# A second level of Strassen's scheme inside the product P3 of each two groups (first products of both SwiGLUs, and the projections)

## The chip, the cores and the metric

The kernel runs on one core of one Trainium2 chip. The metric is the device time of one execution in microseconds; the number given is the median of three runs. A core has a matrix engine (TensorE: PE for its matmuls, PEld for its weight loads), a vector engine (VectorE: DVE), a scalar engine (ScalarE: ACT), and queues that start DMA transfers (here all on SyncE: SP). Each engine works through its own list of instructions in order, and semaphores hold an instruction back until what it needs is there. Matmuls add up in PSUM, eight banks of 128 x 512 fp32; everything else lies in SBUF.

## What is computed

One layer on 1024 tokens of width 1024, in fp32: a SwiGLU with a half-weight residual, a mixing sub-layer (retention and pooling branches behind one combined projection, then gates and an output projection), a second SwiGLU, and a final norm.

```
h = h + 0.5 * swiglu_ffn(rmsnorm(h, norm_ffn1), ffn1_w_in, ffn1_w_out)
u = rmsnorm(h, norm_mix)
proj = u @ w_in                      # 1024 -> 7168: q, k, v, g_ret, p, gates
...                                  # rotary, retention, pooling, gates
h = h + merged @ w_out
h = h + 0.5 * swiglu_ffn(rmsnorm(h, norm_ffn2), ffn2_w_in, ffn2_w_out)
out = rmsnorm(h, norm_final)

def swiglu_ffn(x, w_in, w_out):      # 1024 -> 2 * 2816 -> 1024
    gate, up = jnp.split(x @ w_in, 2, axis=-1)
    return (jax.nn.silu(gate) * up) @ w_out
```

## The kernel before

**Tiling.** Activations lie transposed: channels on the 128 partitions, 1024 tokens along the free dimension. A product takes a 128x128 block of weights as the stationary operand and 512 tokens as the moving one. Every fp32 operand is split into a high and a low part: `split` lets ACT write the high part (a cast, L146) and DVE the rest (L147); `mm3` (L166 to L168) then issues three matmuls, high x high, high x low, low x high. So one 128x128 block on 512 tokens is three matmuls of 128x512.

**Groups and Strassen.** The first products of the SwiGLUs (`ffn_in`) and the projections (`projections`) are cut in groups of 2 x 128 output rows: gate and up of one slice, or two slices of a projection. A group is the product of a 2x2 matrix of weight blocks (L11, L12, L21, L22, each 512 channels in, 128 out) with a 2x2 matrix of activation blocks (R11, R12, R21, R22, each 512 channels by 512 tokens). `strassen` computes it by the Winograd form: seven products in place of eight, P1 to P7, each of 4 x 3 = 12 matmuls of 128x512. Its sums of weights are S1 = L21 + L22, S2 = S1 - L11, S3 = L11 - L21 and S4 = L12 - S2, made on DVE (L365) for every group; the sums of activations T1 to T4 are made once for a stage by the class `Next`, and all seven operands of a stage (4 tiles each) stay in SBUF, in 28 buffers with the tag "mv". The product P3 = S4 x R22 is the last term of one quarter of the result: it is added in PSUM to what bank `b` holds (`b3`), and the bank is then read out by `evac((0, 1), ...)`: on DVE with the factor of the norm (L527 in the SwiGLUs), or by ACT as a copy.

**Order.** `in_turn` yields the steps of the groups: the first two groups of a stage product by product in alternation, the others one after another in the order P1, P7, P6, P2, P5, P4, P3. The first SwiGLU begins with one group without Strassen (`plain_group`). `Flow.run` calls a step's preparation (loads, sums, splits of weights) four steps ahead of its matmuls; after each step it takes one or two pieces of background work (`flow.add`: norm factors, gates, rotary, stores) from a queue. A scheduler then puts the instructions of each engine in a fixed order. All DMAs stand in the one queue of SP, in order.

**Buffers.** PSUM: six banks with the tag "ps" (`bank`) and two with the tag "sum" (`sum_bank`); `b` is a "sum" bank, `a` and `e` are "ps" banks. SBUF: five split weights ("wt"), four raw weight tiles ("raw"), nine tiles of 128x1024 ("t4"), four more ("tl"), eight of 128x512 ("c2"). The "tl" tiles are used by `ffn_out` for the operands that it loads back (`p1` loads `R[k]` into one), by the rotary tables, and by the retention units for q, k and v.

Of the kernel before, what the change touches and what calls it, by code (L numbers as in the profile page):

```python
# [48 lines left out]
N_PS, N_SUM, N_IDLE = 6, 2, 6  # L49
# [40 lines left out]
def block_kernel(ctx: ExitStack, tc, x, x_tok, vecs, f1_in, f1_out, w_in, pool_w, w_ret, w_pool, w_o,  # L90
# [156 lines left out]
    class Next(Norm):  # L247


        def __init__(self, name, gain, keep=None):  # L250
            super().__init__(name)
            self.gain, self.keep = gain, keep
            self.M, self.tiles, self.t1s, self.rb = {}, {}, {}, None
# [70 lines left out]

        def work(self, *steps):

            for f in steps:
                for i in range(4):
                    flow.add(lambda f=f, i=i: f(i))
# [23 lines left out]
    def strassen(nx, wa, wb, name, evac, end, begin=None):  # L353
# [13 lines left out]
        def prep_w(n):  # L367
            def go():
                if n == "L11":
                    blocks()  # L370
                elif n == "S2":
                    combine("S1", "L21", "L22", ADD)
                    combine("S2", "S1", "L11", SUB)
                elif n == "S3":
                    combine("S3", "L11", "L21", SUB)
                elif n == "S4":
# [60 lines left out]
        def last(f):  # L437
            def go():
# [7 lines left out]
        return [(prep_w("L11"), b1), (prep_w("S2"), b6), (prep_w("S1"), b5), (prep_w("S3"), b7),  # L446
                (prep_w("L12"), b2), (prep_w("S4"), last(b3)), (prep_w("L22"), last(b4))]

    def in_turn(groups, order=range(7), first=2):

        groups = list(groups)
        steps = [g() for g in groups[:first]]
        for n in order:
            for g in steps:
                yield g[n]

        for g in groups[first:]:
            steps = g()
            for n in (0, 3, 1, 4, 2, 6, 5):
                yield steps[n]  # L460
# [18 lines left out]
    def plain(M, nk, src, name, evac, begin=None):  # L479

        t = {}
        for q in range(0, nk, 4):
# [27 lines left out]
    def ffn_in(nx, w, ops, name, start=None):  # L510
# [3 lines left out]

        def group(g):
            gate_up = []

            def evac(which, in0, in1):
                if not gate_up:
                    new = tl if start and g == 0 else t4  # L520
                    gate_up.extend((new(f"{name}g{g}"), new(f"{name}u{g}")))
                tile, j = which
                dst = half(gate_up[tile], j)
                if in1 is not None:
                    tt(dst, in0, in1, ADD)
                elif nx.rb is not None:
                    tt(dst, in0, half(nx.rb, j), MUL)  # L527
                    return
                else:
                    copy(dst, in0)  # L530
                flow.add(lambda: tt(dst, dst, half(nx.rms(), j), MUL))

            def end():
# [5 lines left out]
                def times(j):  # L539
                    tt(half(up, j), half(gate, j), half(up, j), MUL)  # L540

                flow.add(swish, lambda: times(0), lambda: times(1))
                hid[g] = up
# [3 lines left out]
                lo, hi, e = hid.pop(k), up, {}  # L547
                R11, R12, R21, R22 = half(lo, 0), half(lo, 1), half(hi, 0), half(hi, 1)

                def w1():  # L550
                    e["n"], e["m"] = t4(f"{name}n{k}"), c2(f"{name}m{k}")
                    tt(half(e["n"], 0), R12, R11, SUB)
                    tt(half(e["n"], 1), R22, R12, SUB)
                    load(B[k], e["n"])

                def w2():
                    tt(R12, R22, half(e["n"], 0), SUB)
# [3 lines left out]
                def w3():  # L561
                    tt(e["m"], R21, R12, SUB)
# [7 lines left out]
            return lambda: strassen(nx, w[g, 0], w[g, 1], f"{name}{g}_", evac, end)  # L570
# [3 lines left out]
        if start:  # L574
            return chain(group(0), in_turn((group(g) for g in order[1:]), (0, 4, 1, 2, 3, 5, 6)))
        return in_turn((group(g) for g in order), BY_OPERAND)
# [237 lines left out]
    first.work(first.r11, first.r21, first.r12, first.r22, first.p22, first.t2, first.t1, first.t3, first.t4_)  # L814
# [9 lines left out]
    first.stats(x_sums)  # L824

# [14 lines left out]
    def end_of(nx):  # L840
        def end(part):
            if part == 0:
                nx.work(nx.r11, nx.r22, nx.t2, nx.t1, nx.t3, nx.p22)
            else:
                nx.work(nx.r21, nx.t4_)
                nx.stats()
# [11 lines left out]
    def rotary_tables():  # L858
        for n, z in (("cos", 0), ("sin", 1)):
            raw_t = tl(f"{n}raw")  # L860
            load(raw_t, rope[z])
            tab[n] = t4(n)
            tt(tab[n], raw_t, mix.rms(), MUL)

    def project(kind, n):
# [87 lines left out]
        def end():  # L953
            if kind in "qk":
                flow.add(*rotate(0), *rotate(1), lambda: keep(qs if kind == "q" else ks))
                if (kind, n) == heavy[-1]:
                    flow.add(units[0].loads)
# [8 lines left out]
        return lambda: strassen(mix, w_in[at], w_in[at + 1], name, evac, end)  # L966
# [5 lines left out]
    def projections():  # L972
        for n, step in enumerate(in_turn(project(*o) for o in order)):
            if n == 28:
# [7 lines left out]
    def pool(n):  # L982
# [12 lines left out]
        def body():  # L995
            for i in range(2):
                mt = 2 * n + i
                dst = [f(f"px{mt}{j}") for j, f in enumerate((sum_bank, bank))]
# [214 lines left out]
    def retention():  # L1213
# [7 lines left out]

        yield units[0].operands, units[0].values
# [34 lines left out]
    def after(nx):  # L1257
# [5 lines left out]
        return {0: nx.r11, 4: nx.r21, 1: t2, 3: nx.t3, 2: nx.t1, 6: nx.t4_, 5: nx.p22}  # L1263
# [75 lines left out]
    def merge():  # L1339
        yield from two_by_two(two_groups(0) + two_groups(1), BY_OPERAND, handed(mg, lambda rest: flow.add(*rest)))  # L1340
        yield from two_by_two((out_group(i) for i in range(4)), BY_OPERAND,
                              handed(ffn2, lambda rest: (flow.add(*rest[:4]), ffn2.stats(between=rest[4:]))))
# [117 lines left out]
```

## Time and profile before

| | |
|---|---|
| median of 3 runs | 2192.77 us (2190.7 to 2193.43) |
| the profiled execution | 2192.35 us, of which its span is 2190.6 us |
| ACT busy | 985.3 us (45%) |
| DMA | 311.86 MB, mean 142 GB/s |
| mean granted TensorE clock | 0.997 |

The page gives each engine's busy time, a picture of the span in 40 slices, the chain of work that ended last and the costliest groups. In a group, the name left of the arrow is what is written; then come the shape, the count, the busy time, the mean duration of one and the idle time ahead of it. The stages by the tiles' names: first SwiGLU 0 to 644 us (its first products to 434), projections 644 to 1175, retention and pooling to 1386, merge and output projection to 1541, second SwiGLU from there on (its first products to 1964). In the names, `a` and `c` are the groups of the two SwiGLUs' first products, `n1`, `n2`, `n3` their operands and those of the projections, `b` and `d` their second products.

### The profile page before, as it was taken

The page shows a single profiled execution, that of the slowest core. Times are in us where ns is not written, and L with a number is a line of the kernel's source. Part 1 is how long each engine was busy: PE and PEld are TensorE (multiplying, and loading weights), DVE is VectorE, ACT ScalarE, POOL GpSimd, SP SyncE. Part 2 cuts the span into 40 slices and gives each one's busy share as a digit, 9 for nine tenths or more (in the row PEclk, how much of TensorE's full clock was granted, in tenths as well). Part 3 has the DMA queues.
Part 4 walks back from the last instruction along what each step waited for, and adds up shares of the span by engine and source line. Part 5 has one row for each costly group of instructions (what it writes and reads, how often), then busy time and mean ns, then how long its engine had stood idle before and what let it go on. Part 6 is the DMA issues. An engine that isn't in the chain of part 4 may idle for free.

```text
span 2190.6 us, 27454 instructions
## 1 busy us (share of the span) xinstructions
PE 2171.6 (99%) x10070; PEld 1809.5 (83%) x10070; DVE 1677.5 (77%) x2766; ACT 985.3 (45%) x1756; POOL 0.2 (0%) x4
## 2 busy tenths in 40 slices
PE   9999999999999999999999999999999999999998
PEld 7788888888888888888888998878888888888887
DVE  8687777887786767677776777799977777689775
ACT  8433333444553433434336664446533333344451
POOL 0000000000000000000000000000000000000000
PEclk9999999999999999999999999999999999999999
DMA  6144222495323333323235557524242323249522
GB/s 239 58 154 168 92 104 96 162 334 178 125 92 112 139 116 116 115 105 127 96 124 187 188 180 278 192 87 147 75 144 101 135 92 123 94 158 337 173 73 78
DMA packets 111015, 311.86 MB, mean 142 GB/s; under 512 B 12448, under 2 KB 14624, under 8 KB 110880
## 3 DMA queue, kind: packets, MB, share of 16 engines
q1 hardware_dynamic: 110880, 310.11, 40.0%
q8 instruction: 79, 1.29, 0.2%
q14 instruction: 56, 0.46, 0.1%
HBM read 219.36 MB, written 90.70 MB: 142 GB/s over the span
## 4 chain that ended last, share of the span: by engine, by line
PE 94%; DVE 3%; ACT 2%; DMA 1%; issue 0%; SPq 0%; DVEq 0%; ACTq 0%
PE c_b L166 3%; PE c_b L168 3%; PE c_b L167 3%; PE a_b L168 2%; PE a_b L166 2%; PE a_b L167 2%; PE c_e L166 2%; PE c_a L167 2%; PE c_a L166 2%; PE c_a L168 2%; PE c_e L168 2%; PE c_e L167 2%; PE a_e L168 2%; PE a_e L167 2%; PE a_a L168 2%; PE a_e L166 2%
## 5 line engine op out<-in xcount | busy, mean ns | idle before, releaser
L146 ACT CAST c_wS<-c_S 128x512 fp32r<-128x512 f32 x88 | 54.7, 622 | 124.7 <-PE c_b L168 76.1
L146 ACT CAST a_wS<-a_S 128x512 fp32r<-128x512 f32 x84 | 52.2, 622 | 105.7 <-PE a_b L168 71.0
L147 DVE TENSOR_TENSOR c_wS<-c_S,c_wS 128x512 fp32r<-128x512 f32 x88 | 60.9, 692 | 22.6 <-ACT c_wS L146 22.0
L147 DVE TENSOR_TENSOR a_wS<-a_S,a_wS 128x512 fp32r<-128x512 f32 x84 | 58.2, 693 | 24.4 <-ACT a_wS L146 24.0
L167 PE MATMUL c_a<-n3R,c_wL 128*128 128x512 f32 x176 | 68.6, 390 | 0.0
L167 PE MATMUL c_b<-n3T,c_wS 128*128 128x512 f32 x176 | 68.5, 389 | 0.0
L168 PE MATMUL c_b<-n3T,c_wS 128*128 128x512 f32 x176 | 68.5, 389 | 0.0
L168 PE MATMUL c_a<-n3R,c_wL 128*128 128x512 f32 x176 | 68.5, 389 | 0.0
L166 PE MATMUL c_a<-n3R,c_wL 128*128 128x512 f32 x176 | 68.3, 389 | 0.0
L166 PE MATMUL c_b<-n3T,c_wS 128*128 128x512 f32 x176 | 68.2, 389 | 0.0
L168 PE MATMUL a_a<-n1R,a_wL 128*128 128x512 f32 x168 | 65.4, 389 | 0.0
L166 PE MATMUL a_a<-n1R,a_wL 128*128 128x512 f32 x168 | 65.4, 389 | 0.0
L167 PE MATMUL a_a<-n1R,a_wL 128*128 128x512 f32 x168 | 65.4, 389 | 0.0
L166 PE MATMUL a_b<-n1T,a_wS 128*128 128x512 f32 x168 | 65.4, 389 | 0.0
L167 PE MATMUL a_b<-n1T,a_wS 128*128 128x512 f32 x168 | 65.4, 389 | 0.0
L168 PE MATMUL a_b<-n1T,a_wS 128*128 128x512 f32 x168 | 65.4, 389 | 0.0
L146 ACT CAST c_wL<-c_ra 128x512 fp32r<-128x512 f32 x44 | 27.2, 620 | 38.0 <-PE c_e L168 38.0
L146 ACT CAST a_wL<-a_ra 128x512 fp32r<-128x512 f32 x42 | 26.0, 621 | 37.6 <-PE a_e L168 37.6
L167 PEld LDWEIGHTS c_a<-n3R,c_wL 128*128 128x128 f32 x176 | 33.0, 188 | 7.2 <-DVE n3R L151 0.3
L167 PEld LDWEIGHTS c_b<-n3T,c_wS 128*128 128x128 f32 x176 | 33.0, 188 | 7.0 <-DVE n3T L151 0.2
L147 DVE TENSOR_TENSOR c_wL<-c_ra,c_wL 128x512 fp32r<-128x512 f32 x44 | 30.4, 692 | 10.8 <-ACT c_wL L146 10.5
L168 PEld LDWEIGHTS c_a<-n3R,c_wL 128*128 128x128 f32 x176 | 33.0, 188 | 6.9
(2500 smaller groups left out, 7300.3 us busy)
## 6 DMA issues: line engine op xcount, KB each, us to landing
c_ra<-in_f_in SPq DMA_DIRECT2D x22, 512.0 KB, 3.7
c_rb<-in_f_in SPq DMA_DIRECT2D x22, 512.0 KB, 4.7
a_ra<-in_f_in SPq DMA_DIRECT2D x21, 512.0 KB, 4.5
a_rb<-in_f_in SPq DMA_DIRECT2D x21, 512.0 KB, 5.1
t<-au SPq DMA_DIRECT2D x11, 512.0 KB, 2.6
b<-an SPq DMA_DIRECT2D x11, 512.0 KB, 3.2
r<-au SPq DMA_DIRECT2D x11, 512.0 KB, 3.8
br<-r SPq DMA_DIRECT2D x11, 512.0 KB, 5.4
```

The lines of the kernel that those rows point to most:

```text
L146: copy(hi, src)
L147: tt(lo, src, hi.bitcast(F32), SUB)
L166: mm(dst, w[0], m[0], start=start, stop=False, skip_group_check=True)
L167: mm(dst, w[0], m[1], start=False, stop=False, skip_group_check=True)
L168: mm(dst, w[1], m[0], start=False, stop=stop, skip_group_check=True)
```

## The change

Two groups A and B now share their P3. S4 of A and S4 of B, one above the other, are a 2x2 matrix of blocks (2 groups x 2 halves of the channels, each 256 in and 128 out), R22 is one of 2 x 2 blocks of 256 channels by 256 tokens, and their product is made by the same Winograd form again: seven products, each of 2 x 3 = 6 matmuls of 128x256. Before, the two P3 were 24 matmuls of 128x512; now they are 42 of 128x256.

- **Weights** (`third`): S4 itself is no longer split. Split are S4 of A (`wx`), two pairs of sums (`ws12`, `ws34`, from four DVE operations of 128x256, L507 to L514) and half of S4 of B (`wy`).
- **Operands** (`Next.quads`): x00, x10, x01, x11 are the quarters of R22, y1 = x01 - x00, y2 = x11 - y1, y4 = x10 - y2, y3 = x11 - x01. They take the place of the four split tiles of R22. Three lie in "mv"; x00, x10, y1 and x11 take all four "tl" buffers for the whole stage, x01 one of "t4".
- **Partial sums**: the products x00, y1 go to a bank `x`, y2 and y3 to a bank `y`, x10 and x11 straight onto bank `b` of A, y4 onto bank `b` of B. ACT copies x00's half of `x` to `y`, and `y`'s one half to its other, between the products; DVE and ACT collect the rest in two SBUF tiles `z` (L529 to L552), which `evac((0, 1), b, z)` adds on the way out (DVE, L663), the norm's factor following as an operation of its own.
- **Order**: `pairs` yields A's six other products, B's six, and then the three steps of `third` with 18, 12 and 12 matmuls. The first pair of a stage goes in alternation as before. In the first SwiGLU the plain group, nine pairs, one group alone (`third_alone`: P3 as 24 matmuls of 128x256 on the four quarters) and one pair; 14 pairs in the projections, 11 in the second SwiGLU: 35 pairs.
- **Elsewhere**: five "ps" banks and three "sum" banks; the pooling products write two "sum" banks instead of one of each; the first group's gate and up lie in "mv"; the rotary tables are loaded straight into "t4"; the first retention unit loads q, k and v at the start of the retention, behind which two pooling products stand, no longer during the projections; the preparation of R22 as an operand is gone from the projections and the second SwiGLU.

```diff
-N_PS, N_SUM, N_IDLE = 6, 2, 6
+N_PS, N_SUM, N_IDLE = 5, 3, 4
...
+        def quads(self):
+            both = [slice(z * HD, (z + 1) * HD) for z in range(2)]
+            x = {(i, j): [self.tiles[4 + 2 * i + z, 1][:, both[j]] for z in range(2)] for i in range(2) for j in range(2)}
...
+            return [block(0, 0), block(1, 0), difference("y1", (0, 1), (0, 0)), difference("y2", (1, 1), "y1"), block(1, 1),
+                    difference("y4", (1, 0), "y2"), difference("y3", (1, 1), (0, 1))], block(0, 1)
...
+        def prep1():
+            w["x"] = weights(a["S4"], f"{A.name}wx")
+            s = t["s"] = c2(f"{A.name}s12")
+            tt(s[:, LO], b["S4"][:, LO], b["S4"][:, HI], ADD)
+            tt(s[:, HI], s[:, LO], a["S4"][:, LO], SUB)
+            w["s12"] = weights(s, f"{A.name}ws12")
...
+        def prod(dst, n, at, m, start=False):
+            for z in range(2):
+                mm3(dst, parts(w[n], at + z), nx.quad(m, z), start and z == 0, z == 1)
+
+        def one():
+            x, y = t["x"], t["y"] = bank(f"{A.name}x"), sum_bank(f"{A.name}y")
+            a["z"], b["z"] = c2(f"{A.name}z"), c2(f"{B.name}z")
+            prod(x[:, LO], "x", 0, "x00", True)
+            with soon():
+                copy(y[:, LO], x[:, LO])
+                copy(a["z"][:, LO], x[:, LO])
+            prod(a["b"][:, LO], "x", 2, "x10")
+            prod(x[:, HI], "s12", 0, "y1")
+            with soon():
+                copy(b["z"][:, HI], x[:, HI])
+
+        def two():
+            y = t["y"]
+            prod(y[:, LO], "s12", 2, "y2")
+            with soon():
+                copy(y[:, HI], y[:, LO])
+                tt(a["z"][:, HI], y[:, LO], b["z"][:, HI], ADD)
+            prod(a["b"][:, HI], "s34", 2, "x11")
+            with soon():
+                A.third()
+
+        def three():
+            y = t["y"]
+            prod(b["b"][:, LO], "y", 0, "y4")
+            prod(y[:, HI], "s34", 0, "y3")
+            with soon():
+                copy(b["z"][:, LO], y[:, HI])
+                tt(b["z"][:, HI], y[:, HI], b["z"][:, HI], ADD)
+                B.third()
...
-                    t["dst"] = [f(f"{name}d{j}") for j, f in enumerate((sum_bank, bank))]
+                    t["dst"] = [sum_bank(f"{name}d{j}") for j in range(2)]
...
+        yield units[0].loads, none
+        yield from fill(2)
         yield units[0].operands, units[0].values
```

Three places where the change moves rows. The rows are the fixed order of one engine, with the semaphores that a row waits for; the numbers at the names tell buffers apart.

On PE, in a pair in the middle of the second SwiGLU, P3 of one group before (bank `b`, operand R22 in four `n3R` tiles):

```order
L166 MATMUL c_b<-n3R_13424,c_wS_14723 128x512 [waits DVE_49]
L167 MATMUL c_b<-n3R_13424,c_wS_14723 128x512
L168 MATMUL c_b<-n3R_13424,c_wS_14723 128x512
L166 MATMUL c_b<-n3R_13427,c_wS_14723 128x512
L167 MATMUL c_b<-n3R_13427,c_wS_14723 128x512
```

and now the middle of the first step of `third` at that place: the end of x10 (`n3x_14726`, onto bank `b`), the first matmul of y2 (`n3y_14770`, onto bank `y`), and y1 (`n3y_14757`, onto the second half of bank `x`):

```order
L167 MATMUL c_b<-n3x_14726,c_wx 128x256
L168 MATMUL c_b<-n3x_14726,c_wx 128x256
L166 MATMUL c_y<-n3y_14770,c_ws_16007 128x256 [waits Activation_49]
L166 MATMUL c_x<-n3y_14757,c_ws_16007 128x256 [waits Activation_49]
L167 MATMUL c_x<-n3y_14757,c_ws_16007 128x256
L168 MATMUL c_x<-n3y_14757,c_ws_16007 128x256 [waits DVE_49]
```

The scheduler has put one matmul of y2 ahead of y1; both wait for ACT, where P3 waited for no one between its matmuls.

On ACT, at that same place, now (`c_wL`, `c_wS` are weights of the next pair):

```order
L146 CAST c_wL_16066<-c_ra 128x512 [waits DMAHW4_49,PE_49,Activation_49]
L529 COPY c_y<-c_x 128x256 [waits PE_49]
L530 COPY c_z<-c_x 128x256
L146 CAST c_wS_16085<-c_S_16083 128x512 [waits DVE_49,PE_49,Activation_49]
L534 COPY c_z<-c_x 128x256 [waits PE_49]
L540 COPY c_y<-c_y 128x256 [waits PE_49]
```

Four copies, of which the first, second and fourth stand between PE's products; before, ACT had nothing to do between the matmuls of a P3. The order is the same in all pairs but the first of a stage.

On SP, at the end of the first SwiGLU's first products, the loads for `ffn_out` now (`br` is the "tl" tile of `p1`, `bra` and `bL22a` are weights):

```order
L134 DMA bra_4030<-in_f_out 128x1024 [waits DMAHW4_49,DVE_49]
L134 DMA bra_4083<-in_f_out 128x1024 [waits DMAHW5_49,DVE_49]
L134 DMA br_3964<-r_123 128x1024 [waits DMAHW6_49,PE_49]
L134 DMA br_4028<-r_124 128x1024 [waits DMAHW7_49,PE_49]
L134 DMA br_4081<-r_125 128x1024 [waits DMAHW0_49,PE_49]
L134 DMA br_4142<-r_126 128x1024 [waits DMAHW1_49,PE_49]
```

and before, the piece with the fifth of these loads, the first that waits for a buffer:

```order
L134 DMA bra_3555<-in_f_out 128x1024 [waits DMAHW0_49,DVE_49]
L134 DMA br_3712<-r_126 128x1024 [waits DMAHW1_49,DVE_49]
L134 DMA bra_3603<-in_f_out 128x1024 [waits DMAHW2_49,DVE_49]
L134 DMA bL22a_3605<-in_f_out 128x512 [waits DMAHW6_49,DMAHW7_49,DMAHW3_49,DVE_49]
L134 DMA bra_3671<-in_f_out 128x1024 [waits DMAHW5_49,DVE_49]
```

Before, the first four `br` stood far ahead of this piece, since nothing else held the four "tl" buffers; now the first four wait for PE, for the last pair's x00, x10, y1 and x11 to be done.

More of the change, by code (lines that the diff above doesn't have):

```diff
@@ L462, in two_by_two, with alone @@
+    def alone(nx, group):
+        A = group()
+        for m in BY_SUM:
+            yield A[m]
+        yield third_alone(nx, A)
     def two_by_two(groups, order, between=None):
@@ L824, in block_kernel @@
     first.stats(x_sums)
+    quads, x01 = first.quads()
+    flow.add(*quads, x01)
     ops1 = spill("r", FH), spill("t", FH), spill("b", FH), spill("m", FH, H)
@@ L972, in projections @@
     def projections():
[L973 to L974 removed]
+        for n, step in enumerate(pairs(mix, (project(*o) for o in order), (0, 1, 2, 3, 4, 6))):
+            if n == 30:
                 flow.rate = 1
```

132 lines of the change are left out of this document (95 added, 37 removed).

## Prediction

> **What bounds the kernel now.** First the page: the span, the busy times and the chain that ended last.
>
> ```profile
> span 2190.6 us, 27454 instructions
> PE 2171.6 (99%) x10070; PEld 1809.5 (83%) x10070; DVE 1677.5 (77%) x2766; ACT 985.3 (45%) x1756; POOL 0.2 (0%) x4
> PE 94%; DVE 3%; ACT 2%; DMA 1%; issue 0%; SPq 0%; DVEq 0%; ACTq 0%
> ```
>
> PE is busy for 99% of the span, and 94% of the chain is PE's. So a matmul less is time less, as long as nothing else becomes late. Who could become late is read from the three stages that change, in the view of windows (us, then the busy time of PE, PEld, DVE, ACT and POOL, each with its number of instructions, PE's granted clock, the DMA share, GB/s):
>
> ```profile
> 0.00:434.00 434.00, 429.50 (x1875) 352.25 (x1876) 330.20 (x529) 192.40 (x315) 0.20 (x4) 1.00 0.37 132
> 644.00:1175.00 531.00, 531.00 (x2347) 438.96 (x2346) 384.63 (x605) 216.05 (x379) 0.00 (x0) 1.00 0.32 118
> 1541.00:1964.00 423.00, 423.00 (x1869) 348.97 (x1868) 323.30 (x512) 166.65 (x271) 0.00 (x0) 1.00 0.31 110
> ```
>
> PE has no gap in two of them (531.00 of 531.00, 423.00 of 423.00) and 4.5 us in the first. The clock is whole. DVE is next: 323.30 of 423 us in the second SwiGLU, 76%. ACT has room. DVE decides whether the change pays.
>
> **The change: matmuls.** The gain hangs on what a matmul of half the width costs. The timeline of PE (start, duration, instruction) shows a run of the full width, and two runs of the half width, from other stages:
>
> ```profile
> 1759.79 0.39 PE L166 MATMUL c_e<-n3T,c_wS 128*128 128x512 f32 x1
> ...
> 1760.24 0.39 PE L168 MATMUL c_e<-n3T,c_wS 128*128 128x512 f32 x1
> 1760.47 0.39 PE L166 MATMUL c_b<-n3T,c_wS 128*128 128x512 f32 x1
> 2155.05 0.28 PE L168 MATMUL dp6b<-dp4m,dp4w 128*128 128x256 f32 x1
> ...
> 2165.49 0.28 PE L168 MATMUL dp6b<-dp4m,dp4w 128*128 128x256 f32 x1
> 1193.01 0.28 PE L166 MATMUL ob<-v,sm 128*128 128x256 f32 x1
> ...
> 1194.93 0.28 PE L168 MATMUL ob<-v,sm 128*128 128x256 f32 x1
> ```
>
> The spacing counts, not the duration, since matmuls are pipelined. Full width: 0.68 us for three steps, 0.2267 each. Half width: 10.44 us for 87 steps of an output product, 0.120; 1.92 us for 17 steps in the retention, 0.113. So the half is a little more than half. I take 0.118, near the long run.
>
> The order of PE loses 852 matmuls of 128x512 (35 pairs x 24, and 12 of the group that is alone) and gains 1494 of 128x256 (35 x 42 + 24). Removed: 852 x 0.2267 = 193.1 us. Added: 1494 x 0.118 = 176.3. **Balance -16.8 us**; -13.8 at 0.120, -24.3 at 0.113. A pair goes from 24 x 0.2267 = 5.44 us to 42 x 0.118 = 4.96: a gain of 0.48, out of 168 x 0.2267 = 38.1 us.
>
> The Trainium skill, page "TensorE: Matmul & The Clock Gate", section "Back-to-back issue gap", gives for a single matmul N / 2.4 + 2.5 ns, which would be 215.8 ns at 512 and 109 at 256, an estimate of 183.9 - 162.8 = 21 us from that page. The rows show 226.7 and 113 to 120, so the measurement decides.
>
> **y1 waits for ACT.** x00 goes to one half of bank `x`, y1 to the other, and in the fixed order y1 stands behind both copies that ACT makes of x00. What such a step costs is read at other hand-overs (the first ACT row follows the c_e row of 1760.24 above):
>
> ```profile
> 1760.67 0.59 ACT L419 COPY c_p<-c_e 128x512 f32<-128x512 f32 x1 [1.61 <-PE c_e L168]
> 1761.15 0.62 ACT L146 CAST c_wS<-c_S 128x512 fp32r<-128x512 f32 x1
> 1195.53 0.69 ACT L146 CAST state<-sf 128x512 fp32r<-128x512 f32 x1
> 1196.27 0.19 PEld L166 LDWEIGHTS xb<-state,q 128*128 128x128 f32 x1 [1.26 <-ACT state L146]
> 1196.27 0.38 PE L166 MATMUL xb<-state,q 128*128 128x256 f32 x1 [1.06 <-ACT state L146]
> ```
>
> ACT starts 0.04 us after the recorded end of the last matmul (1760.24 + 0.39 = 1760.63). A second ACT instruction starts 0.11 before the first one's end (1760.67 + 0.59 = 1761.26, next 1761.15). PE starts 0.05 after ACT's end (1195.53 + 0.69 = 1196.22, then 1196.27), and the first matmul after a wait takes 0.38 instead of 0.28. A copy of 256 columns out of PSUM is not in the trace; it is bounded by its neighbours (groups: count, busy, mean ns, idle before):
>
> ```profile
> L397 ACT COPY c_b<-c_a 128x512 f32<-128x512 f32 x22 | 12.6, 571 | 21.6 <-PE c_a L168 21.6
> L402 ACT COPY c_v<-c_b 128x512 f32<-128x512 f32 x22 | 12.9, 587 | 27.4 <-PE c_b L168 27.4
> L146 ACT CAST c_wS<-c_S 128x512 fp32r<-128x512 f32 x88 | 54.7, 622 | 124.7 <-PE c_b L168 76.1
> L146 ACT CAST sm<-sc 128x256 fp32r<-128x256 f32 x8 | 3.3, 407 | 4.9 <-DVE sc L1105 4.9
> ```
>
> A cast loses 622 - 407 = 215 ns by halving; so 571 - 215 = 0.36 us for the copy to `y`, 587 - 215 = 0.37 for that to `z`.
>
> Now with x00's start as 0: its sixth matmul starts at 5 x 0.118 = 0.59 and ends at 0.87; copy y from 0.91 to 1.27 (the cast of `wL` ahead of it on ACT is done by then); copy z from about 1.18 to 1.55; y1's weights from 1.60. Without a wait y1 would start after x00, x10 and the one matmul of y2 that stands ahead: 13 x 0.118 = 1.53. With the 0.1 of a first matmul that is 1.70 against 1.53, **0.16 us** per pair in round figures. At 33 pairs in steady order (35 without the first ones of two stages) that is **+5.3 us**. From below 0 (a faster copy), from above 0.35 us (each copy a full 0.57, without overlap nearly twice that, but y2's matmul hides part): 0 to 11.5 us. What is behind the wait: all of PE, so it counts in full.
>
> The Trainium skill, page "PSUM — Partial Sum Buffer", section "PSUM bank collisions raise a hardware error", says that two engines may not be on one bank at once even at different columns. That speaks against putting x00 and y1 on one bank: without the rule y1 need not wait, the term is 0 and the time 2178.5. No run here shows a collision; the wait stands in the order all the same.
>
> **DVE's additions.** The prices, by groups and one pair of neighbours:
>
> ```profile
> L147 DVE TENSOR_TENSOR c_wS<-c_S,c_wS 128x512 fp32r<-128x512 f32 x88 | 60.9, 692 | 22.6 <-ACT c_wS L146 22.0
> L147 DVE TENSOR_TENSOR sm<-sc,sm 128x256 fp32r<-128x256 f32 x8 | 3.4, 423 | 0.2
> L527 DVE TENSOR_TENSOR cg<-c_b,n3rb 128x512 f32<-128x512 f32 x22 | 15.2, 691 | 13.0 <-PE c_b L168 12.9
> 1761.80 0.69 DVE L147 TENSOR_TENSOR c_wS<-c_S,c_wS 128x512 fp32r<-128x512 f32 x1 [1.42 <-ACT c_wS L146]
> 1762.41 0.68 DVE L365 TENSOR_TENSOR c_S<-c_ra,c_rb 128x512 f32<-128x512 f32 x1
> ```
>
> Per pair come one split of 512 (0.69) and one of 256 (0.42), six sums of 256 (6 x 0.42 = 2.5), and two more read-outs of 512, since adding `z` and multiplying by the norm's factor are two operations (2 x 0.69): 5.0 us. The operands of `quads` add 7.1 us to a stage. In the second SwiGLU DVE then needs 323.3 + 11 x 5.0 + 7.1 = 385 of 418 us, 92%. I cost this at nothing, because the order puts DVE's work ahead of its use. The nearest date inside the third is y3, which needs the sum of L541, since that reads the other half of bank `y`. In DVE's order six operations lead up to it, of which the first, an evac, starts when PE is done with `e`, at 0.2 (x00's start is 0): five spacings of 0.61 us (1761.80 to 1762.41) and its own 0.42 make it ready at 3.7, and 4.0 with a wait for a cast; PE needs it after 36 matmuls and y1's wait, at 36 x 0.118 + 0.16 = 4.4. The cover is **0.4 us**; beyond it each delay of DVE is PE's. The next one is the split of the next group's S2, four operations on, ready at 4.0 + 4 x 0.61 = 6.4 and needed after the third and two products, at 4.96 + 0.16 + 24 x 0.2267 = 10.6.
>
> ACT gets two casts (0.62 + 0.41) and five copies (5 x 0.37), 2.9 us per pair: 166.65 + 32 of 418, room enough.
>
> **The starts of the second products.** `ffn_out` runs twice. Its first four `br` tiles now wait for the last pair's x00, x10, y1 and x11:
>
> ```profile
> L134 SPq DMA_DIRECT2D br<-r x11: 320/326/927, 131.9 to 464.7; - x11
> DMA to landing us min/median/max: 3.2/5.4/9.0
> PE a_b L166 <- DVE au L525: 2.2, 1, 2.2
> ```
>
> Behind the first free tile, x00's, stand 36 matmuls of the third, 4.3 us. A landing takes 3.2 / 5.4 / 9.0 us (minimum, median, maximum), and its cast 0.62. So 0 at best; 5.4 + 0.6 - 4.3 = 1.7 at the median, 9.0 + 0.6 - 4.3 = 5.3 at the most, if the first product needed it at once, which it doesn't: its `br` stands behind the last group's read-out and the weights. I take 0.5 each, 1 us (0 to 4, twice a median landing and a little). In the first pair of the first SwiGLU a wait of 2.2 us for DVE is there already (last row); with the operands of R22 made on DVE nearby I add 1 us (0 to 2). The pooling products write banks "sum" back to back, where the second must wait for the read-out of an earlier one; the retention's first loads have two pooling products as cover: 1 us (0 to 2). Together **+3 us** (0 to 8).
>
> **Sum**, against the profiled execution's own time, 2192.35 us (0.42 under the median of the runs): 2192.35 - 16.8 + 5.3 + 3.0 = 2183.9; on the median's scale 2184.3. **I say 2184.0.**
>
> **Rivals.**
>
> *All of it hidden.* y1's wait and the starts cost nothing: 2192.35 - 16.8 = 2175.5, at 0.113 per matmul 2168. For it: PE's sequencer has 13 matmuls between x00 and y1, so a wait of 0.16 rests on estimates of 0.05; against it: the long run of half-width matmuls shows 0.120.
>
> *The gain is eaten.* The change does not do what it says: 42 half-width matmuls cost as much as 24 whole ones at 24 / 42 x 0.2267 = 0.1295 us, or at 0.120 with a y1 wait at its bound: 2192.35 - 13.8 + 11.5 + 3 = 2193. For it: a pair's gain, 0.4 to 0.48, is as small as one hand-over between engines, and the third has four of them. Against it: 87 steps at 0.120 without one lost. Between 2189 and 2193.
>
> *DVE becomes the bound: slower.* The view of waits gives DVE's idle time in the second SwiGLU (total, times, longest):
>
> ```profile
> DVE cu L525 <- PE c_b L168: 23.9, 18, 1.3
> DVE c_wS L147 <- ACT c_wS L146: 22.0, 22, 1.4
> DVE c_wL L147 <- ACT c_wL L146: 16.7, 27, 0.8
> DVE cg L527 <- PE c_b L168: 12.9, 18, 0.7
> ```
>
> These are 75.5 us, 6.9 a pair. DVE's work will be 29.4 (323.3 / 11) + 5.0 + 0.6 = 35.0 us a pair, PE's 37.6. Waits of up to 2.6 us a pair are free. If 4 of the 6.9 stay, because evac and casts come from PE and ACT in turn however late DVE is, DVE takes 39: a loss of 1.4 us x 21 SwiGLU pairs = 29, that is 2204.6. It decides from a loss of 0.4 us a pair, where the sum's gain of 8.4 is gone (8.4 / 21), and from 0.63 it is slower by more than can be measured (8.4 + 0.4 + 4.4, over 21). Against it: waits shrink when their engine falls behind, and the longest is 1.4 us, inside DVE's lead of 4 (10.6 - 6.4).
>
> **How the numbers follow.** Forecast (2179 to 2188.4) 0.47; all hidden (2168 to 2179) 0.21; eaten (2188.4 to 2195) 0.17; DVE the bound (2195 to 2208) 0.15. The range leaves out the lower end of the hidden case and most of the last: **2172 to 2195**. A measurement of this kernel tells about 0.2% from no change, 4.4 us: same is 2188.4 to 2197.2. Faster takes the first two, 0.68; same is the third, 0.17; slower is the last, 0.15, whose few tenths under 2197.2 I leave there.
>
> **What would show it.** Right: PE's matmul count 642 higher; half-width matmuls 0.117 to 0.120 apart inside a product; a gap on PE of 0.1 to 0.2 us ahead of y1 and none ahead of y2, x11, y4 and y3; PE's list of waits grown by about 8 us, y1's the first row, by ACT; DVE busy above 90% in the second SwiGLU's first products without PE waiting for a weight (L147) there. Wrong: rows of PE waiting for DVE's L147, L541 or an evac in each pair (DVE bounds); a spacing over 0.125; gaps of several us at the first product of `ffn_out` or at the retention's start; a granted clock under 1.00 in a stage.

## The result and the profile after

| | before | after |
|---|---|---|
| median | 2192.40 us (4 runs, 2190.7 to 2193.43) | 2219.38 us (4 runs, 2217.78 to 2221.15) |
| profiled execution | 2192.35 us | 2220.38 us |
| ratio | | 1.0124, 95% interval 1.0106 to 1.0142 |

The change makes the kernel 1.2% slower, 27 us, where 8 us less were forecast. The page of the changed kernel, the lines that answer to those shown of before:

```profile
span 2218.4 us, 29495 instructions
PE 2181.2 (98%) x10712; PEld 1833.2 (83%) x10712; DVE 1824.1 (82%) x3164; ACT 1065.6 (48%) x2009; POOL 0.2 (0%) x4
PE 89%; DVE 6%; DMA 2%; ACT 1%; issue 1%; SPq 0%; DVEq 0%; ACTq 0%
```

PE has 642 matmuls more, as counted in the order (10712 - 10070). Its share of the chain falls from 94 to 89%, and DVE's doubles. So the time went where PE waits for others, and the next step is to find where. A table of stage lengths does that: from the timeline of PE, the start of a stage's first matmul to the start of the next one's (retention with the pooling; "merge" with the output projection; the last stage to the end of its last matmul), in us, one profiled execution each. The kernels below the second row are those of the experiments.

```
                 SwiGLU 1         projec-  reten-  merge   SwiGLU 2
                 first   second   tions    tion            first   second
before           428.19  209.44   536.93   205.36  155.41  423.09  219.31
after            431.93  215.63   534.00   211.82  156.31  428.61  227.32
z_from_y         428.84  216.42   533.51   208.28  155.41  427.80  227.12
first_alone      424.33  218.10   534.11   208.52  156.63  421.69  228.00
tl_free3         430.64  217.50   534.01   208.56  156.71  433.05  219.60
pool_banks       430.26  217.37   534.01   207.60  156.75  429.26  228.05
all_mended       424.57  209.47   533.46   209.56  155.45  418.63  220.09
all_mended_banks 424.37  209.47   533.49   207.15  155.44  419.21  219.53
proj_only        426.92  209.44   534.00   207.99  155.41  423.30  219.00
loads_early      423.96  209.46   534.53   205.19  155.41  418.63  220.04
places_only      425.11  209.46   534.52   205.15  155.40  418.65  219.56
```

(Stages that an edit doesn't touch show how far one execution can be from the next: 215.6 to 218.1 in the first SwiGLU's second products and 208.3 to 211.8 in the retention, for the same code.) The second products and the retention have the same products as before, and yet became 6.2, 8.0 and 6.5 us longer. The first products, which have less to compute, became 3.7 and 5.5 us longer. Only the projections gained.

**Inside the stages the pairs are fast.** From the start of one pair's `third` (its shared P3) to the next it is 37.86 us in both SwiGLUs (7 of 7 and 9 of 9 such distances behind the first, within 0.04), against 38.08 for two groups before: 0.22 us gained per pair. And VectorE is not full there. The view of windows, 38 us in the middle of the second SwiGLU, after:

```profile
1752.00:1790.00 38.00, 38.00 (x188) 32.22 (x187) 30.66 (x52) 16.02 (x29) 0.00 (x0) 1.00 0.32 105
```

and before:

```profile
1753.00:1791.00 38.00, 38.00 (x169) 31.49 (x168) 27.46 (x43) 13.75 (x23) 0.00 (x0) 1.00 0.29 104
```

DVE went from 27.5 to 30.7 of 38 us (81%), and PE is busy throughout. The stretch of the first pair's `third` in the same stage is another picture, after:

```profile
1590.00:1606.00 16.00, 10.05 (x51) 6.89 (x50) 15.49 (x38) 8.17 (x18) 0.00 (x0) 1.00 0.00 1
```

PE works 10.05 of 16 us, DVE 15.49. The timeline of PE names what it waits for there (idle time before a row, and what ended it):

```profile
1593.52 0.39 PE L166 MATMUL c_x<-n3y,c_ws 128*128 128x256 f32 x1 [1.38 <-ACT n3y L146]
...
1596.24 0.38 PE L166 MATMUL c_y<-n3y,c_ws 128*128 128x256 f32 x1 [0.53 <-ACT n3y L146]
...
1597.52 0.39 PE L167 MATMUL c_y<-n3y,c_ws 128*128 128x256 f32 x1 [0.90 <-DVE n3y L147]
...
1598.84 0.39 PE L166 MATMUL c_b<-n3y,c_wy 128*128 128x256 f32 x1 [0.46 <-ACT n3y L146]
...
1601.79 0.39 PE L167 MATMUL c_y<-n3y,c_ws 128*128 128x256 f32 x1 [1.16 <-DVE n3y L147]
```

Each wait is for an operand `n3y`: y1, y2, y4, y3 are still being made while their products are due. And the same place of the kernel before:

```profile
1571.00:1590.00 19.00, 19.00 (x81) 14.99 (x80) 18.91 (x38) 9.59 (x14) 0.00 (x0) 1.00 0.14 46
```

DVE had 18.91 of 19.00 us of work there already, and the change adds its 7.1 us of operands just there. This row was to be had before the prediction.

**At the second products the lead is gone.** These are the loads of the operand that `p1` loads (`dr` in the second SwiGLU) and ACT's casts of it, eleven each, with the start of the first and the last; before, where the stage begins at 1964.57:

```profile
L134 SPq DMA_DIRECT2D dr<-r x11: 319/327/1128, 1600.6 to 1995.5; - x11
L146 ACT CAST dp1m<-dr x11: 603/617/626, 1946.5 to 2003.4; 128x512 fp32r<-128x512 f32 x11
```

and after, where it begins at 1984.40:

```profile
L134 SPq DMA_DIRECT2D dr<-r x11: 320/327/944, 1980.1 to 2029.2; - x11
L146 ACT CAST dp1m<-dr x11: 613/617/623, 1983.7 to 2036.2; 128x512 fp32r<-128x512 f32 x11
```

The first load moved from 1600.6 to 1980.1, four us ahead of the stage, and the first cast from 18 us ahead to 0.7. SP's queue around it shows what stood behind that load (a row with x4 is four in a piece):

```profile
1963.75 4.23 SPq L134 DMA_DIRECT2D dra<-in_f_out  x2
1980.10 3.36 SPq L134 DMA_DIRECT2D dr<-r  x4
1987.43 0.81 SPq L134 DMA_DIRECT2D dL22a<-in_f_out  x2
...
2008.69 3.97 SPq L134 DMA_DIRECT2D dacc<-h  x6
2012.77 2.28 SPq L134 DMA_DIRECT2D dL22a<-in_f_out  x2
```

The weights `dL22a` come from the same queue and stand behind the four `dr`. Two of them that start here at 2012.77, 28.4 us into the stage, started before only 15.8 us into it:

```profile
1980.40 1.70 SPq L134 DMA_DIRECT2D dL22a<-in_f_out  x2
```

The bill comes 40 us into the stage, in the timelines of DVE and PE:

```profile
2023.71 0.69 DVE L787 TENSOR_TENSOR ds<-dra,dL22a 128x512 f32<-128x512 f32 x1 [6.50 <-DMA dL22a<-in_f_out]
```

```profile
2025.91 0.50 PE L166 MATMUL dp6b<-dp6m,dp6w 128*128 128x512 f32 x1 [3.62 <-ACT dp6w L146]
...
2027.70 0.63 PE L167 MATMUL dp6b<-dp6m,dp6w 128*128 128x512 f32 x1
2028.13 0.63 PE L168 MATMUL dp6b<-dp6m,dp6w 128*128 128x512 f32 x1
```

DVE waits 6.50 us for weights, PE 3.62 us behind it, and then PE runs at 0.43 us a matmul for a while (see the last section). That the late weights stem from the four loads ahead of them is read from the order of the queue; the experiment tl_free3 below tests it.

So the theory for the experiments: the loss is at the starts, in three separate places. The first pair's operands come late (theory one), the "tl" buffers hold the next stage's loads and the queue (theory two), and something lengthens the retention. The rival for all: VectorE is too full in any order, and what is mended in one place comes back in the next.

### The profile page after: what moved, and what is told of

It reads as the page before. It is cut to its first block, busy times and chain, and to the rows that moved or that the text cites. A ratio compares the mean times of both kernels' runs of the same rounds, so it can differ in the third digit from the quotient of the medians.

```text
span 2218.4 us, 29495 instructions
## 1 busy us (share of the span) xinstructions
PE 2181.2 (98%) x10712; PEld 1833.2 (83%) x10712; DVE 1824.1 (82%) x3164; ACT 1065.6 (48%) x2009; POOL 0.2 (0%) x4
## 4 chain that ended last, share of the span: by engine, by line
PE 89%; DVE 6%; DMA 2%; ACT 1%; issue 1%; SPq 0%; DVEq 0%; ACTq 0%
PE c_b L166 2%; PE c_b L167 2%; PE c_b L168 2%; PE a_b L167 2%; PE a_b L166 2%; PE a_b L168 2%; PE c_a L167 2%; PE c_a L166 2%; PE c_e L166 2%; PE c_a L168 2%; PE c_e L168 2%; PE c_e L167 2%; PE a_a L167 2%; PE a_a L166 2%; PE a_a L168 2%; PE a_e L168 2%
## 5 line engine op out<-in xcount | busy, mean ns | idle before, releaser
L146 ACT CAST c_wS<-c_S 128x512 fp32r<-128x512 f32 x66 | 41.0, 622 | 70.1 <-DVE c_S L411 56.5
L146 ACT CAST a_wS<-a_S 128x512 fp32r<-128x512 f32 x64 | 39.7, 622 | 64.7 <-DVE a_S L411 39.2
L147 DVE TENSOR_TENSOR c_wS<-c_S,c_wS 128x512 fp32r<-128x512 f32 x66 | 45.1, 684 | 2.6 <-ACT c_wS L146 1.2
L147 DVE TENSOR_TENSOR a_wS<-a_S,a_wS 128x512 fp32r<-128x512 f32 x64 | 43.7, 685 | 1.4
L167 PEld LDWEIGHTS c_a<-n3R,c_wL 128*128 128x128 f32 x176 | 33.1, 188 | 7.0 <-DVE n3R L151 0.3
L168 PEld LDWEIGHTS c_a<-n3R,c_wL 128*128 128x128 f32 x176 | 33.0, 188 | 7.0
L168 PEld LDWEIGHTS c_b<-n3T,c_wS 128*128 128x128 f32 x176 | 33.0, 188 | 6.9
L166 PEld LDWEIGHTS c_a<-n3R,c_wL 128*128 128x128 f32 x176 | 33.1, 188 | 6.8 <-issue 0.2
L166 PEld LDWEIGHTS c_b<-n3T,c_wS 128*128 128x128 f32 x176 | 33.0, 188 | 7.0 <-ACT n3T L146 0.2
L167 PEld LDWEIGHTS c_b<-n3T,c_wS 128*128 128x128 f32 x176 | 33.0, 188 | 6.8
```

Source lines behind the costliest of these rows:

```text
L146: copy(hi, src)
L147: tt(lo, src, hi.bitcast(F32), SUB)
L166: mm(dst, w[0], m[0], start=start, stop=False, skip_group_check=True)
L167: mm(dst, w[0], m[1], start=False, stop=False, skip_group_check=True)
L168: mm(dst, w[1], m[0], start=False, stop=stop, skip_group_check=True)
```

## The experiments

**z_from_y.** The term of y1, by itself: the second copy of x00 reads what the first one wrote, so that ACT is on bank `y` while PE goes on in bank `x`.

```diff
                 copy(y[:, LO], x[:, LO])
-                copy(a["z"][:, LO], x[:, LO])
+                copy(a["z"][:, LO], y[:, LO])
```

> The copy of x00 into z reads bank y instead of bank x. Theory 'y1 waits for the second copy': the distance from one pair's third to the next goes from 37.86 us to about 37.69 in the steady pairs, as long as from x00 to y1 without a gap; 33 x 0.17 = 5.6 us less in all, about 2213.8. Rival 'the gap belongs to the change of bank or weights, or y2 waits instead': 37.86 stays and 2219.4 too.

2212.2 us in its one run (one run of before beside it, and beside the next three experiments, took 2192.57). Of the 7 us against after, 3.6 are 21 pairs of the SwiGLUs by 0.17; most of the rest is the scatter of the retention. In the SwiGLUs the distance is 37.68 to 37.69 in every steady pair. In the table the second SwiGLU gained only 0.8 of its share: behind the first pair's waits TensorE's granted clock fell to 0.50 there, from 1588 to 1598 us, which it doesn't in after. The timeline of PE at this place, after (the last matmul of x10, the one of y2, then y1):

```profile
1980.50 0.28 PE L168 MATMUL c_b<-n3x,c_wx 128*128 128x256 f32 x1
1980.62 0.28 PE L166 MATMUL c_y<-n3y,c_ws 128*128 128x256 f32 x1
1980.81 0.39 PE L166 MATMUL c_x<-n3y,c_ws 128*128 128x256 f32 x1
1981.03 0.28 PE L167 MATMUL c_x<-n3y,c_ws 128*128 128x256 f32 x1
```

and of z_from_y, where the scheduler puts no matmul of y2 ahead of y1 any more:

```profile
1972.40 0.28 PE L168 MATMUL c_b<-n3x,c_wx 128*128 128x256 f32 x1
1972.52 0.28 PE L166 MATMUL c_x<-n3y,c_ws 128*128 128x256 f32 x1
1972.64 0.28 PE L167 MATMUL c_x<-n3y,c_ws 128*128 128x256 f32 x1
```

After, the two steps around y1's first matmul take 0.19 and 0.22 in place of 0.12, in z_from_y 0.12 each: y1's wait was ACT's second copy, and it was 0.17 us. A change of bank without a wait costs nothing that shows (`c_b` to `c_x` above, 0.12). In the projections, though, most distances stay at 37.8 to 37.9. There the wait has moved, as the timelines of ACT and DVE show:

```profile
992.99 1.15 ACT L1064 ACTIVATE t7B<-t7B,vec 128x1024 f32<-128x1024 f32 x1
994.04 0.35 ACT L534 COPY t7z<-q2x 128x256 f32<-128x256 f32 x1
994.30 0.38 ACT L540 COPY q2y<-q2y 128x256 f32<-128x256 f32 x1
994.71 0.42 DVE L541 TENSOR_TENSOR q2z<-q2y,t7z 128x256 f32<-128x256 f32 x1 [0.37 <-ACT q2y L540]
```

A gate's sigmoid of 1.15 us stands ahead of ACT's copies. The copy L540 comes late by it, DVE's sum L541 waits for that copy and ends at 995.13, and y3 waits for the sum. PE's last matmul of y4 starts at 994.94, the first two of y3 at 995.18 and 995.41: two steps of 0.24 and 0.23 where 0.12 is the rule. So the theory holds in the SwiGLUs; in the projections the distance stays, as the rival had it, but by a wait of y3 that neither named.

**first_alone.** In both SwiGLUs the first pair makes its P3 the plain way, on the four quarters, so that the four differences are due only 38 us later; they also stand behind x01 and x11 in the order of making. In the second SwiGLU x01, which the change doesn't make there, now lies in an "mv" buffer.

```diff
-                if n == "x01":
+                if n == "x01" and self.name == "n1":
...
+            if n == 0 and by_self:
+                yield third_alone(nx, A)
+                yield third_alone(nx, B)
+            else:
+                yield from third(nx, A, B)
...
-    flow.add(*quads, x01)
+    flow.add(quads[0], quads[1], x01, quads[4], *quads[2:4], *quads[5:])
```

> The first pair of both SwiGLUs makes its two P3 as 24 matmuls of half width each on x00, x10, x01, x11, so that y1 to y4 are needed only with the second pair. Theory 'the start is lost to operands that come late': the first products of the second SwiGLU go from 428.6 us to 421.5 to 424 (7.9 us of loss at the start gone, 0.55 us for the 6 more matmuls), those of the first SwiGLU from 431.9 to 427 to 429. Rival 'VectorE has too much to do there in any order': both stay within 1.5 us.

2206.07 us in one run. The first products became 424.33 and 421.69 us, 7.6 and 6.9 less than after, and now below before. In the second SwiGLU that is what theory one says; in the first it is 2.7 us more than it had: the 2.2 us wait for DVE that the kernel before has in its first pair, and the stretch of half the clock behind that (last section), are not there in this kernel. The window with PE's 10.05 of 16 us, and the same place of the stage, which begins 8.0 us earlier here, read in this kernel

```profile
1582.00:1598.00 16.00, 15.34 (x87) 12.69 (x86) 15.92 (x38) 7.77 (x15) 0.00 (x0) 1.00 0.20 64
1590.00:1606.00 16.00, 15.34 (x64) 11.71 (x63) 14.97 (x31) 9.60 (x15) 0.00 (x0) 1.00 0.20 66
```

with DVE as full as ever (15.92 and 14.97) and PE at work. Theory one holds: VectorE's work was not too much, PE asked for it too early. Nothing of it clearly came back in the second products: 228.00 against 227.32, and 218.10 against 215.63 in the first SwiGLU, where kernels with the same code there have up to 217.5.

**tl_free3.** In the second SwiGLU alone three of the four operands leave the "tl" buffers: y1 to the last free "mv" buffer, x00 and x10 to "t4". The first SwiGLU is the control.

```diff
-                if n in ("x00", "x10", "y1", "x11"):
+                if n in ("x00", "x10", "y1", "x11") and not (self.name == "n3" and n in ("y1", "x00", "x10")):
                     return sb.tile([P, 2, H], F32R, tag="tl", bufs=N_TL, name=name)
-                if n == "x01":
+                if n == "x01" or self.name == "n3" and n in ("x00", "x10"):
```

> In the second SwiGLU alone y1 lies in the last mv buffer and x00 and x10 in t4 buffers, so that three of the four tl buffers are free for the first loads of the second product. Theory 'the loads wait for buffers, and the queue behind them': its second products go from 227.3 us to 219 to 222, those of the first SwiGLU stay at 215.6. Rival 'VectorE's work at the end of the last pair': 226 to 228 stays.

2215.07 us in one run. The second products of the second SwiGLU are back at 219.60 us (before 219.31), those of the first SwiGLU stay at 217.50. The first load and the first cast are early again:

```profile
L134 SPq DMA_DIRECT2D dr<-r x11: 319/326/1263, 1631.7 to 2023.5; - x11
L146 ACT CAST dp1m<-dr x11: 615/619/624, 1967.2 to 2030.4; 128x512 fp32r<-128x512 f32 x11
```

The stage starts at 1986.92 here, so the cast is 19.7 us ahead. Theory two holds; the edit frees the buffers and with them the queue, so it doesn't part the two. The price shows in the column beside it: the first products became 4.4 us longer (433.05). PE's first product with x10 starts 44 us into the stage there, behind a late cast (1597.68; 35 us in after); that "t4" still holds tiles of the previous stage and x10 waits for them is argued, not tested. A part of the 4.4 us is the clock, 0.50 from 1592.4 to 1602.7 and from 1606.1 to 1609.5, which in after is whole there.

**pool_banks.** The pooling products write one "sum" and one "ps" bank again, as before the change (the same edit stands at the products `px`).

```diff
-                    t["dst"] = [sum_bank(f"{name}d{j}") for j in range(2)]
+                    t["dst"] = [f(f"{name}d{j}") for j, f in enumerate((sum_bank, bank))]
```

> The pooling products write one sum bank and one ps bank again. Theory 'two sum banks back to back wait for the read-out': the retention goes from 211.8 us to about 208, without the wait ahead of pu5 (2.0 us and the slow matmuls behind it). Rival 'the gates come late there, whatever the banks': 211 to 212 stays.

2218.38 us in one run; the retention 207.60. That is 4.2 less than after, but only 0.7 to 1.0 less than three kernels that leave the banks alone (208.28 to 208.56). The wait ahead of pu5 (1.8 us after) is 0.3 us in first_alone without this edit, so much of the 211.8 was that one execution's. Inconclusive alone.

**all_mended** and **all_mended_banks.** The edits together. The operands got places by stage, with y2 and y3 in "t4" in the second SwiGLU, where they are made late now, and x10, x11 in "tl", y4 in "t4" in the first (n1, n2, n3 are the first SwiGLU, the projections and the second SwiGLU; what isn't named lies in "mv"):

```diff
+PLACES = {'n1': {'x11': 'tl', 'x10': 'tl', 'x01': 't4', 'y4': 't4'}, 'n2': {'x00': 'tl', 'x10': 'tl', 'y1': 'tl', 'x11': 'tl', 'x01': 't4'}, 'n3': {'x01': 'tl', 'y2': 't4', 'y3': 't4', 'y4': 'tl'}}
...
+                at = PLACES[self.name].get(n, "mv")
```

> The three edits that helped alone, together: z read from bank y, the first pair's P3 of both SwiGLUs as 24 + 24 matmuls on the quarters, and buffers placed so that in the second SwiGLU three, in the first two of the four tl buffers are free for the first loads of the second products. Theory 'the three losses are apart and add up': first products 422 to 424 and 419 to 421 us, second products 210 to 212 and 219 to 221, in all 2184 to 2188, less than before. Rival 'one delay behind all of them, on VectorE': an edit's gain comes back in the next stage, 2195 or more.

> The same with one sum bank and one ps bank for the pooling products again. Theory 'the sum banks back to back are a part of the retention's loss': 1 to 2 us less than the kernel without it. Rival 'they are not': the same within 1 us.

Measured: 2187.05 us for all_mended (10 runs; ratio to before 0.9979, interval 0.9970 to 0.9989), 2183.74 for all_mended_banks (4 runs; 0.9962, 0.9948 to 0.9977), against 2192.0 for before (19 runs). Every stage of the SwiGLUs is within 0.6 us of the range that theory has for it, the total of all_mended is inside, and the gains add up: the losses were apart. PE's list of waits in all_mended_banks has no row of the thirds' operands or of the second products at its head, only the old ones and one of y3:

```profile
PE fin2b L227 <- DVE fin2dg L226: 2.0, 1, 2.0
PE wo1b L167 <- ACT wo1wS L147: 1.6, 1, 1.6
PE fin2sum L216 <- DVE n4ssq L246: 1.6, 1, 1.6
PE a_y L167 <- DVE a_z L541: 1.3, 1, 1.3
```

The banks' part is 2.4 us in the retention (209.56 to 207.15, one execution each) and 3.3 us between the medians, more than either theory had.

**proj_only.** The second level in the projections alone; the SwiGLUs make P3 as before, everything else stays as in the change.

> The second level in the projections alone; both SwiGLUs make P3 as before, with the split R22; banks, pooling and the retention's loads as in the change. Theory 'the loss lies at the starts of the SwiGLUs' stages': their four stages go back to 428.2, 209.4, 423.1 and 219.3 us within 1 us, the projections stay at 534.0, the retention at 208 to 212: 2192 to 2197 in all. Rival 'fewer ps banks and the moved loads cost it everywhere': the SwiGLUs' stages stay 3 us or more above those of before.

2191.33 us (10 runs), ratio 1.000 (0.999 to 1.001). Three of the SwiGLUs' stages are back within 0.4 us of before (209.44, 423.30, 219.00), the fourth lies 1.3 below it (426.92), so the five "ps" banks cost them nothing that shows. Of the 2.9 us that the projections gain, 2.6 are spent in the retention (207.99 against 205.36).

**loads_early** and **places_only.** Where the retention's rest comes from. Both put the projections' x10 and x11 in "t4" and y1 in "mv", which leaves three "tl" buffers free; loads_early also moves the call for the retention's first loads back into the projections.

```diff
-          'n2': {'x00': 'tl', 'x10': 'tl', 'y1': 'tl', 'x11': 'tl', 'x01': 't4'},
+          'n2': {'y1': 'mv', 'x00': 'tl', 'x10': 't4', 'x11': 't4'},
...
-        yield units[0].loads, none
-        yield from fill(2)
...
+                if (kind, n) == heavy[-1]:
+                    flow.add(units[0].loads)
```

> all_mended_banks with the projections' operands placed so that three tl buffers stay free (x10 and x11 in t4, y1 in mv), and the retention's first loads back during the projections, without the two pooling products as cover. Theory 'the rest of the retention's loss comes from the moved loads and the pooling products ahead of it': the retention goes from 207.2 us to 205.0 to 205.8, in all 1 to 2 us less than all_mended_banks. Rival 'the loss is in the banks': 207 stays. If two t4 buffers less hold the projections up, their 533.5 us grow.

> The same places of the projections' operands, but the retention's first loads where the change put them. Both theories: the retention stays at 207 to 208 us; the projections stay at 533.5 if the two t4 buffers are not needed.

2182.61 us (5 runs; ratio 0.9963, 0.9949 to 0.9977) and 2183.31 (5 runs; 0.9962, 0.9949 to 0.9975), against 2191.37 for before (9 runs). The retention is 205.19 and 205.15 us: back at 205.36 in both. What I expected of places_only was wrong. The moved call costs nothing; that the buffers are free does it, 2.0 us against all_mended_banks. It is the same kind of cause as at the second products. The projections pay 1.0 us for the two "t4" buffers (534.5 against 533.5), so in all it is a draw with all_mended_banks.

## Why the prediction was wrong

The forecast was 2184.0, in a range of 2172 to 2195; measured were 2219.4. Its steps, one by one:

- **The matmuls** were near right, 3 us too much: -16.8 us at 0.118 us for a half-width matmul. The steps of `third` run at 0.120 (from 1979.19 to 1980.62 in the changed kernel are 12 steps, 0.119 each; the rest keeps 0.12), which was a bound given with it, -13.8. Here the long run of 87 steps was the better row.
- **y1's wait** was right in mechanism and size: 0.16 expected, 0.17 measured, taken away in the SwiGLUs by the edit that names its cause. (The 33 pairs of the sum should be 32, as each of the three stages has a first pair; that is 0.2 us.) ACT's second copy read bank `y` then, and there was no wait in the SwiGLUs. The rule of the Trainium skill, page "PSUM — Partial Sum Buffer", section "PSUM bank collisions raise a hardware error", fits that: with ACT's second copy on another bank than PE's product the order needs no wait, though no run here shows a collision.
- **The cover of 0.4 us at y3** was right in the SwiGLUs (L541 ends at 1982.81 + 0.43 = 1983.24, y3 starts at 1983.66). In the projections it isn't there in z_from_y, as ACT is late behind a gate.
- **DVE costed at nothing** was right in the pairs, and its share was put too high even: 81% in the middle of the stage and 82% over all of it (352.9 of 428.6 us), not 92. It was wrong in the first pair of both SwiGLUs. The step that failed is the division of a stage's busy time by its pairs: 385 of 418 us is an average over a full start and a loose middle. First pair of the second SwiGLU: 428.61 - 423.09 = 5.5 us, plus the 11 x 0.22 = 2.4 gained in its pairs, is a loss of 7.9; of the first SwiGLU 3.7 + 10 x 0.22 - 0.2 (for the group alone, 24 x 0.12 against 12 x 0.2267) = 5.7. The sum had 1 us for the first SwiGLU, nothing for the second. first_alone, which lets PE ask for the differences one pair later, took 7.6 and 6.9 us away.
- **The starts of the second products** had 1 us (0 to 4), and took 6.2 + 8.0. This step failed too. It priced one landing against the 36 matmuls behind x00. It left out that SP works in order: the next weights stood behind the four loads, and a lead of 18 us that all later steps lived on was gone. With three "tl" buffers free the second SwiGLU's loss is 0.3 us (219.60 against 219.31). The order of SP, shown with the change, already had the four in a row behind one another.
- **The retention** had 1 us (0 to 2), and took 6.5 in the profiled execution, 2.9 to 3.2 in three others with the same code there. The "tl" buffers are 2.0 of it (207.15 to 205.15), the banks of the pooling products the rest: 0.7 to 1.0 by pool_banks, 2.4 by all_mended_banks, each from single executions. The term named the banks and the moved loads; the moved loads cost nothing.
- **The sum for the starts** was thus +3 us (0 to 8), and came to 5.7 + 6.2 + 6.5 + 0.9 + 7.9 + 8.0 = 35.2 us, the merge with 0.9 included. Less what the pairs gave (2.0 and 2.4 in the SwiGLUs, 2.9 in the projections) that is 35.2 - 7.3 = 27.9, and the spans differ by 2218.4 - 2190.6 = 27.8. As the losses are read from the stage table, this shows only that none is left out.

The slower rival had the right engine and the wrong place. "DVE becomes the bound" was priced as 1.4 us in each of 21 pairs; there is none of that (37.86 us, pair after pair), and what DVE did cost, 5.7 and 7.9 us, fell in the first pair of each SwiGLU (in the first SwiGLU with a stretch of half the clock behind it). The argument against it, DVE's lead of 4 us, was good for the pairs alone.

With the starts mended the kernel takes 2182.6 to 2183.7 us (all_mended_banks, loads_early, places_only). That the forecast reads 2184.0 is no credit to it: it said so of another kernel.

## What to carry to other kernels

An engine's share over a stage says nothing about its first pair of steps: look at a window of that length at the stage's start, and if the engine is full there, put new work later or let the first step do without it. Buffers that a change holds longer are paid for in the stage that would have loaded into them, and in a queue that works in order by everything behind that load; so list for each such buffer who asks for it next and how far ahead it asked before. A gain of 0.2 to 0.4 us in each of 35 pairs needs every start to cost next to nothing, and it was worth 8 us here once they did.

## What the runs showed of the hardware

A pause of less than 2 us can halve TensorE's clock, and the same pause can leave it whole. In the changed kernel the view of windows (the granted clock is the number behind POOL's count) shows four stretches of half the clock behind a pause, ahead of its last microseconds:

```profile
80.50:85.00 4.50, 4.50 (x13) 3.63 (x12) 3.96 (x8) 1.62 (x3) 0.00 (x0) 0.50 0.18 28
1366.20:1368.00 1.80, 1.80 (x6) 1.36 (x5) 1.80 (x6) 0.00 (x0) 0.00 (x0) 0.50 0.20 77
1492.90:1494.60 1.70, 1.70 (x5) 1.32 (x4) 1.70 (x4) 1.02 (x2) 0.00 (x0) 0.50 0.00 0
2027.60:2030.60 3.00, 3.00 (x8) 2.31 (x8) 3.00 (x6) 1.20 (x4) 0.00 (x0) 0.50 0.90 335
```

At 0.50 a full-width matmul takes 0.427 us in place of 0.227. The pauses ahead of them, from the steps between PE's rows, were 1.0 and 1.4 us within 3 us (at 75 and 77), 2.0 (at 1362), 1.8 (at 1489) and 3.8 (at 2022). But a pause of 3.0 us (at 476) leaves the clock whole in the same kernel, and in the kernel before one of 2.3 us (at 58) halves it:

```profile
478.90:484.00 5.10, 5.00 (x20) 3.71 (x21) 5.10 (x10) 3.19 (x6) 0.00 (x0) 1.00 1.03 395
62.10:65.30 3.20, 3.20 (x9) 2.45 (x9) 1.67 (x5) 0.00 (x0) 0.00 (x0) 0.50 0.00 0
```

The pause of 1.8 us at `wo1b`, in the output projection, is in all eleven kernels. Behind it the clock is halved in four of them (after, first_alone, tl_free3, pool_banks) and whole in seven. One of each, first_alone (halved) and z_from_y (whole):

```profile
1484.00:1487.00 3.00, 2.96 (x7) 2.40 (x8) 3.00 (x6) 1.69 (x3) 0.00 (x0) 0.50 0.00 0
1485.00:1488.00 3.00, 2.58 (x11) 1.82 (x11) 3.00 (x6) 2.21 (x5) 0.00 (x0) 1.00 0.00 0
```

The column "merge" of the stage table has the price: 155.40 to 155.45 us in the seven, 156.31 to 156.75 in the four. So the length alone doesn't decide. A hint of what does lies in the dates. The stretches of the changed kernel begin at 78.37, 1365.20, 1491.49 and 2027.38 us, last 3.41 us (the first 6.83), and the distances between their starts are 377, 37 and 157 times 3.4133 us. So the clock seems to change only at the points of a fixed grid, and how a pause lies on that grid would differ from one execution to the next. No run here tests this.

The Trainium skill, page "TensorE: Matmul & The Clock Gate", section "HAM oscillation — how this bites in real kernels", puts the limit at gaps of more than about 3.4 us; three of the four stretches came behind shorter ones, so here the measurement decides. It means that a wait's price can be more than its length: 3.8 us at 2022, and 7 matmuls of 0.2 us extra, 1.4, behind it.
